# Decay and beta projection of a hybrid encoder: high and low weights in one weight of 64 columns, two passes in place of three

## The chip, the core and the metric

The kernel runs on one core of a Trainium2 chip. The metric is device time: microseconds of one execution, median over runs. TensorE (PE in the profile) has two clock levels, 1.2 and 2.4 GHz; the granted clock of a stretch is shown as a share of the higher one. The other engines are VectorE (DVE), ScalarE (ACT), GpSimd (POOL) and SyncE (SP), which here issues most of the transfers.

## The reference

One trunk layer on 1024 tokens of width 1024, with 16 learned tokens put in front (1040 positions). What the change touches is `ab`, the 32 columns of the input projection that give decay and beta (two directions, 8 heads each):

```python
hn = rms_norm(h, norm_g)
proj = hn @ w_in
f_in, qkv, z, ab, gate_f, gate_d = jnp.split(proj, points, axis=-1)
...
a_f, b_f, a_b, b_b = jnp.split(ab.astype(jnp.float32), 4, axis=-1)
g_f = -jnp.exp(a_log_f) * jax.nn.softplus(a_f + dt_bias_f)
beta_f = jax.nn.sigmoid(b_f)
...
o_fwd = gated_delta_chunked(qp, kp, vp, pad_to_chunks(g_f), pad_to_chunks(beta_f))
```

Everything else (the convolved q, k and v of 8 heads, the chunked delta scan in both directions, the Fourier branch, the two output gates, the router and the mixture of experts) is computed after it and is not edited.

## The kernel before

**Numbers in two parts.** Activations and weights are kept as a rounded high part and a low part, the remainder (`xh`, `xl`, `wh`, `wl`). A product is the sum of three passes: high weight by high input, high weight by low input, low weight by high input. The weight is the stationary operand, so the output stands with its columns on partitions and the tokens along the free axis. One pass over the 1024 inputs is 8 matmuls of 128 rows each, so an output tile takes 24 matmuls. `load_w` (L192) fetches a weight; `split` (L862) makes `wh` with ScalarE (L863) and `wl` with VectorE (L864). `product` (L211) runs the 24 matmuls (all on L220) into a PSUM tile `proj` and calls an evacuation.

**norm1** (L139) loads nine tiles of x (16 learned tokens, then 8 times 128), normalises each (`hn`, L170, VectorE), transposes it on TensorE into PSUM tiles `tp` (L176), and copies these out as `xh` (L178, ScalarE) and `xl` (L179, VectorE). Beside that it runs two projections over the token ranges of `EARLY` (272, 384 and 384 columns): `ab`, with 32 output columns, evacuated by one ScalarE copy into `abT` (L148), and the first tile of k, with 128, evacuated into `pad` (L360). `gates` (L230) turns `abT` into decays and betas for the delta scan, which are written to memory (`dF`) and read back from there.

**The heads** (about 60 to 500 us) project the other tiles of q, k, v with `product`. A projected tile goes from PSUM into `pad` (L360, ScalarE), through a convolution of five taps (first tap L373 on ScalarE, the four others L377 on VectorE, two instructions each, into `acc`), and through SiLU (L350, L351) into `kraw`, `qT` or `vraw`. For each k tile, `k_front` squares and sums transposed blocks (L442), makes the root by a few tiny VectorE and GpSimd instructions (L98 to L109, `rk_y`), and scales them into `ktok` (L450, ScalarE); TensorE transposes these back (L460) and ScalarE copies them into `kT` (L461). `vtok` (L473) is the same for v and is stored by a transfer `dv` (L477), after which its buffer is used again. For each q tile ScalarE squares (`sqq`, L482) and TensorE sums over partitions (L485). `decay` (L489) loads `F` from `dF` (L493), subtracts (L497) and limits it (L498) on VectorE, and takes its exponential on ScalarE (L499); `chunks` (L504) multiplies k by k or q by k (L511). Parts of the triangular inverses (`tmp`, `M`: L691, L693 on VectorE, `M<-dL` transfers L532) run among them.

**What sets the order.** A scheduler places instructions on each engine by its own model of time, outside the delta scan whose TensorE order is written by hand. Each engine then runs its list strictly in order. So fewer or other instructions in norm1 also change the order of instructions that nobody edited. The later parts are the scan (about 500 to 1040 us), projections of the output with router (to about 1250 us, L870 on TensorE) and the experts (weights fetched at L1233 on the SP queue).

Of the kernel before, what the change touches and what calls it, by code (L numbers as in the profile page):

```python
# [8 lines left out]
F32 = mybir.dt.float32  # L9
F32R = mybir.dt.float32r  # L10
BF16 = mybir.dt.bfloat16
I32 = mybir.dt.int32
AF = mybir.ActivationFunctionType
OP = mybir.AluOpType
# [81 lines left out]
def rsqrt(nc, pool, src, shape, scale, eps, tag):  # L96
    x = pool.tile(shape, F32, name=tag + "_x")
    nc.vector.tensor_scalar(x, src, scale, eps, op0=OP.mult, op1=OP.add)  # L98
    return rsqrt_of(nc, pool, x, shape, tag)
# [13 lines left out]
class Kern:  # L113
# [25 lines left out]
    def norm1(self, hp):  # L139

        tc, nc, io = self.tc, self.nc, self.io
        self.xh = hp.tile([128, 8, NT], F32R, name="xh")
        self.xl = hp.tile([128, 8, NT], F32R, name="xl")
        abT = self.tp.tile([32, NT], F32, name="abT", tag="pad")
        pad, ev_k = self.pad_tile()

        def ev_ab(a, b, o):
            nc.scalar.activation(abT[:, a:b], o, AF.Copy)  # L148
        with tc.tile_pool(name="n1", bufs=2) as wp, tc.tile_pool(name="n1p", bufs=self.TB, space=PSUM) as pp:
            xs = []  # L150
            for i in range(9):
                x = wp.tile([128, D], F32, name="x", bufs=9)
                src = io["meta_tokens"] if i == 0 else io["x"][128 * (i - 1):128 * i]
                nc.sync.dma_start(x[:src.shape[0]], src)
                xs.append(x)
                if i == 1:
                    g = wp.tile([128, D], F32, name="g1", bufs=1)
                    nc.scalar.dma_start(g, io["norm1_g"].partition_broadcast(128))
                    nc.gpsimd.dma_start(self.cst[:, :128], io["cst"][:, :128])
                if i == self.JB:  # L160
                    jobs = [(self.load_w(io["w_ab"], 8, 32), 32, ev_ab), (self.load_w(io["w_t"][12], 8, 128), 128, ev_k)]
            for i in range(9):
                n = 16 if i == 0 else 128
                x = xs[i]
                sq = wp.tile([128, D], F32, name="sq", bufs=1)
                ss = wp.tile([128, 1], F32, name="ss")
                nc.scalar.activation(sq[:n], x[:n], AF.Square, accum_out=ss[:n])
                r = rsqrt(nc, wp, ss[:n], [n, 1], 1.0 / D, EPS, "r")
                hn = wp.tile([128, D], F32, name="hn", bufs=self.HB)
                nc.vector.scalar_tensor_tensor(hn[:n], x[:n], r, g[:n], op0=OP.mult, op1=OP.mult)  # L170
                c0 = 0 if i == 0 else 16 + 128 * (i - 1)
                for b in range(2):
                    ps = pp.tile([128, 4, 128], F32, name="tp")
                    for j in range(4):
                        k = 4 * b + j
                        nc.tensor.transpose(ps[:, j, :n], hn[:n, 128 * k:128 * k + 128], self.ident[:n, :n])  # L176
                    oh = self.xh[:, 4 * b:4 * b + 4, c0:c0 + n]
                    nc.scalar.activation(oh, ps[:, :, :n], AF.Copy)  # L178
                    nc.vector.tensor_tensor(self.xl[:, 4 * b:4 * b + 4, c0:c0 + n], ps[:, :, :n],  # L179
                                            oh.bitcast(F32), op=OP.subtract)  # L180
            nc.sync.dma_start(self.cst[:, 128:], io["cst"][:, 128:])
            for r in range(3):
                for w, m, ev in jobs:
                    for _ in self.product(w, m, self.EARLY[r:r + 1], ev):
                        pass
        return abT, pad
# [7 lines left out]
    def load_w(self, src, kt, n):  # L194
# [5 lines left out]
        self.split(wh[:, :kt, :n], wl[:, :kt, :n], wr[:, :kt, :n])  # L200
        return wh, wl

    def project(self, *a):
        for _ in self.project_g(*a):
            pass
# [4 lines left out]

    def product(self, w, n, tiles, evac):  # L211
        nc = self.nc
        wh, wl = w
        for a, b in tiles:
            ps = self.pproj.tile([128, 512], F32, name="proj")
            o = ps[:n, :b - a]
            m = 0
            for k in range(8):
                for w, x in ((wh, self.xh), (wh, self.xl), (wl, self.xh)):
                    nc.tensor.matmul(o, w[:, k, :n], x[:, k, a:b], start=(m == 0), stop=(m == 23))  # L220
                    m += 1
                    if m == 24:
                        evac(a, b, o)
                    yield (b - a) / 2.4

# [1558 lines left out]
```

## Time and profile before

| | |
|---|---|
| time, median of 3 runs | 1783.92 us (1782.64 to 1784.94) |
| profiled execution: its time | 1784.23 us |
| profiled execution: its span | 1782.4 us |
| mean granted TensorE clock | 0.98 |
| busy: PE | 1709.2 us, 96% of the span, 10018 matmuls |
| busy: DVE | 1043.3 us, 59% |
| busy: ACT | 693.9 us, 39% |
| busy: POOL | 195.0 us, 11% |

The span runs from the first to the last instruction; 1.83 us of the profiled execution lie around it. PE counts matmuls, PEld the loads of their stationary operand, which run beside the matmuls. Busy shares are means over stages of very different character: a gain in one stage is read from that stage.

### The profile page before, as it was taken

How to read it: one execution, taken by the hardware profiler on the slowest of the kernel's cores; microseconds unless marked ns; L12 is line 12 of the kernel's file. 1: busy time of each engine (PE TensorE's matmuls, PEld its weight loads, DVE VectorE, ACT ScalarE, POOL GpSimd, SP SyncE). 2: the span in 40 equal slices, each digit the busy share in tenths (PEclk: the TensorE clock that was granted, in tenths of full speed). 3: DMA queues.
4: the chain of work that ended last, by engine and by line, in shares of the span. 5: the costliest groups of instructions: out<-in, count | busy, mean ns of one | idle time of the engine just before them, and what ended most of it. 6: DMA issues, size and time to landing. Idle time of an engine off the chain costs nothing. (4 is left out here: it accounts for less than half of the span.)

```text
span 1782.4 us, 26489 instructions
## 1 busy us (share of the span) xinstructions
PE 1709.2 (96%) x10018; PEld 1222.1 (69%) x10018; DVE 1043.3 (59%) x2198; ACT 693.9 (39%) x1537; POOL 195.0 (11%) x300
## 2 busy tenths in 40 slices
PE   7999999999999997999999999999699999999996
PEld 6999999999788885667666678888443444344342
DVE  6666699999458974565656546623624344424434
ACT  5666575553322113444444433322323333223232
POOL 2000000100100011132332000010201011101100
PEclk9999999999999998999999999999799999999998
DMA  4144643544653458343444067525699999999994
GB/s 162 48 136 158 184 130 131 154 134 135 226 154 130 159 195 219 113 143 101 142 142 123 23 220 249 176 89 202 248 397 420 414 420 418 419 419 415 420 419 192
DMA packets 118670, 391.16 MB, mean 219 GB/s; under 512 B 36439, under 2 KB 38399, under 8 KB 93567
## 3 DMA queue, kind: packets, MB, share of 16 engines
q1 hardware_dynamic: 102312, 337.65, 51.8%
q0 software_dynamic: 14736, 51.02, 9.0%
q8 instruction: 81, 1.33, 0.3%
q10 hardware_dynamic: 1488, 0.73, 0.2%
q14 instruction: 53, 0.43, 0.1%
HBM read 328.28 MB, written 65.26 MB: 221 GB/s over the span
## 5 line engine op out<-in xcount | busy, mean ns | idle before, releaser
L220 PE MATMUL proj<-xh,wh 128*128 128x346 f32 (+5 forms) x1080 | 389.9, 361 | 8.3 <-ACT zt L1699 6.0
L220 PE MATMUL proj<-xl,wh 128*128 128x346 f32 (+4 forms) x1080 | 390.4, 362 | 0.0
L220 PE MATMUL proj<-xh,wl 128*128 128x346 f32 (+4 forms) x1080 | 389.2, 361 | 0.0
L220 PEld LDWEIGHTS proj<-xh,wh 128*128 128x128 f32 (+1 forms) x1080 | 203.7, 189 | 28.2 <-ACT zt L1699 6.4
L220 PEld LDWEIGHTS proj<-xl,wh 128*128 128x128 f32 (+1 forms) x1080 | 203.7, 189 | 18.7 <-issue 5.8
L220 PEld LDWEIGHTS proj<-xh,wl 128*128 128x128 f32 (+1 forms) x1080 | 203.2, 188 | 19.1 <-issue 6.6
L377 DVE SCALAR_TENSOR_TENSOR acc<-pad,convw,acc 128x520 f32<-128x520 f32 x192 | 135.5, 753 | 17.0 <-ACT acc L373 16.9
L863 ACT ACTIVATE wh<-wr 128x1024 fp32r<-128x1024 f32 (+2 forms) x77 | 77.5, 1008 | 144.9 <-PE proj L220 84.0
L864 DVE TENSOR_TENSOR wl<-wr,wh 128x1024 fp32r<-128x1024 f32 (+2 forms) x77 | 88.9, 1156 | 50.5 <-ACT wh L863 42.5
L1346 DVE SCALAR_TENSOR_TENSOR ea<-ea,gw,gu 128x256 f32<-128x256 f32 x32 | 15.4, 481 | 172.4 <-ACT ea L1345 172.4
L691 DVE TENSOR_TENSOR tmp<-M 128x62 f32<-128x62 f32 (+30 forms) x124 | 106.0, 855 | 4.2 <-DMA M<-dL 2.6
L693 DVE TENSOR_TENSOR M<-M,tmp 128x62 f32<-128x62 f32 (+30 forms) x124 | 106.0, 855 | 1.9
L744 DVE SCALAR_TENSOR_TENSOR R<-main,egn,svtok 128x128 f32<-128x128 f32 x128 | 44.9, 351 | 101.5 <-PE main L742 101.5
L753 ACT ACTIVATE vd<-main,vdec 128x128 f32<-128x128 f32 x128 | 46.9, 366 | 137.8 <-PE main L751 137.6
L761 DVE SCALAR_TENSOR_TENSOR S<-S,egl,dS 128x128 f32<-128x128 f32 x240 | 72.6, 344 | 40.2 <-PE dS L760 39.6
L742 PE MATMUL main<-S,skq 128*64 128x128 f32 x1024 | 86.2, 288 | 0.1
L1345 ACT ACTIVATE ea<-gu 128x256 f32<-128x256 f32 x32 | 12.3, 384 | 183.7 <-PE gu L1341 183.7
L1371 DVE TENSOR_TENSOR yl<-dn,yh 128x512 fp32r<-128x512 f32 x64 | 44.2, 691 | 60.4 <-ACT yh L1370 60.3
L1370 ACT ACTIVATE yh<-dn 128x512 fp32r<-128x512 f32 x64 | 38.1, 595 | 97.8 <-PE dn L1368 97.1
L742 PEld LDWEIGHTS main<-S,skq 128*64 128x64 f32 x1024 | 54.7, 137 | 31.0 <-DVE so L764 16.9
L1341 PE MATMUL gu<-ml,gx 128*64 128x512 f32 x288 | 70.7, 607 | 3.6 <-DMA ml<-in_w_gu_dram 3.6
L1341 PE MATMUL gu<-mh,gx 128*64 128x512 f32 x288 | 67.0, 593 | 1.9 <-DMA mh<-in_w_gu_dram 1.9
(432 smaller groups left out, 3147.2 us busy)
## 6 DMA issues: line engine op xcount, KB each, us to landing
mh<-in_w_gu_dram SPq DMA_DIRECT2D x36, 1024.0 KB, 19.7
ml<-in_w_gu_dram SPq DMA_DIRECT2D x36, 1024.0 KB, 21.0
wr<-in_w_t_dram SPq DMA_DIRECT2D x52, 512.0 KB, 3.9
wx<-in_w_gu_dram SPq DMA_DIRECT2D x20, 1024.0 KB, 19.5
mh<-in_w_dn_dram SPq DMA_DIRECT2D x20, 1024.0 KB, 21.1
ml<-in_w_dn_dram SPq DMA_DIRECT2D x18, 1024.0 KB, 19.9
yh<-in_w_gu_dram SPq DMA_DIRECT2D x16, 1024.0 KB, 19.8
yl<-in_w_gu_dram SPq DMA_DIRECT2D x16, 1024.0 KB, 19.9
```

The lines of the kernel that those rows point to most:

```text
L220: nc.tensor.matmul(o, w[:, k, :n], x[:, k, a:b], start=(m == 0), stop=(m == 23))
L377: nc.vector.scalar_tensor_tensor(o, pad[:, a + j:a + j + NT // 2], w[:, j:j + 1], o, op0=OP.mult, op1=OP.add)
L691: nc.vector.tensor_tensor(tv, M[:, j + 1:, j:j + 1].to_broadcast([np_, m, j]), M[:, j:j + 1, :j].to_broadcast([np_, m, j]), op=OP.mult)
L693: nc.vector.tensor_tensor(M[:, j + 1:, :j], M[:, j + 1:, :j], tv, op=OP.add)
L742: nc.tensor.matmul(ps[hs[half], i], kv[:, i, 2 * (p % 4) + half], st[half], start=True, stop=True)
L744: nc.vector.scalar_tensor_tensor(R, ps[:, 0], self.egn[:, col:col + 1], d["vtok"][p // 4][:, p % 4], op0=OP.mult, op1=OP.add)
L753: nc.scalar.activation(vd, ps[:, 2], AF.Copy, scale=self.vdec[:, col:col + 1])
L761: nc.vector.scalar_tensor_tensor(st[half], st[half], self.egl[:, half, col:col + 1], dS, op0=OP.mult, op1=OP.add)
L863: self.nc.scalar.activation(hi, src, AF.Copy)
L864: self.nc.vector.tensor_tensor(lo, src, hi.bitcast(F32), op=OP.subtract)
L1341: nc.tensor.matmul(pg[self.HS[i]], d["x"][:, 4 * kk + k, c:c + 64], w[:, 4 * i + k], start=(kk == 0 and k == 0), stop=(kk == 1 and k == 3))
L1371: nc.vector.tensor_tensor(yl[:, cs], pd, yh[:, cs].bitcast(F32), op=OP.subtract)
```

## The change

`ab` gets one weight of 64 columns, the 32 high parts on the left and the 32 low parts on the right. Two passes over it (high input, low input) leave high weight by input on PSUM partitions 0 to 31 and low weight by input on 32 to 63. ScalarE copies the first half as before, and VectorE adds the second half. The sum has one small term more than before, low by low. Per token range 16 matmuls with 64 output columns take the place of 24 with 32.

```diff
         def ev_ab(a, b, o):
-            nc.scalar.activation(abT[:, a:b], o, AF.Copy)
+            nc.scalar.activation(abT[:, a:b], o[:32], AF.Copy)
+            nc.vector.tensor_tensor(abT[:, a:b], abT[:, a:b], o[32:], op=OP.add)
...
-                    jobs = [(self.load_w(io["w_ab"], 8, 32), 32, ev_ab), (self.load_w(io["w_t"][12], 8, 128), 128, ev_k)]
+                    jobs = [(self.load_ab(), 64, ev_ab), (self.load_w(io["w_t"][12], 8, 128), 128, ev_k)]
...
+    def load_ab(self):
+        w = self.wp.tile([128, 8, 128], F32R, name="wh")
+        self.wp.tile([128, 8, 128], F32R, name="wl")
+        wr = self.wp.tile([128, 8, 128], F32, name="wr")
+        self.nc.sync.dma_start(wr[:, :, :32], self.io["w_ab"])
+        self.split(w[:, :, :32], w[:, :, 32:64], wr[:, :, :32])
+        return w,
...
     def product(self, w, n, tiles, evac):
-        wh, wl = w
+        parts = ((w[0], self.xh), (w[0], self.xl), (w[-1], self.xh))[:1 + len(w)]
...
-                for w, x in ((wh, self.xh), (wh, self.xl), (wl, self.xh)):
-                    nc.tensor.matmul(o, w[:, k, :n], x[:, k, a:b], start=(m == 0), stop=(m == 23))
+                for wk, x in parts:
+                    nc.tensor.matmul(o, wk[:, k, :n], x[:, k, a:b], start=(m == 0), stop=(m == 8 * len(parts) - 1))
```

Line numbers of the changed kernel are one higher from L149 on and ten higher from about L204 on: L220 becomes L230, L377 L387, L450 L460, L482 L492, L497 L507 and so on. Its lists have 24 TensorE instructions fewer and 3 VectorE instructions more, and the scheduler's order differs on all engines up to about 500 us; from there on the lists are practically the same.

**TensorE, the first instructions of norm1.** `tp` are transposes of x, `proj` the projections. Before:

```order
L176 MATMUL tp<-cst,hn 128x16 x8
L176 MATMUL tp<-cst,hn 128x128 x24
L220 MATMUL proj<-xh,wh 32x272
L220 MATMUL proj<-xl,wh 32x272
L220 MATMUL proj<-xh,wh 128x272
L220 MATMUL proj<-xl,wh 128x272
L176 MATMUL tp<-cst,hn 128x128 x8
L220 MATMUL proj<-xh,wl 32x272
```

Now:

```order
L177 MATMUL tp<-cst,hn 128x16 x8
L177 MATMUL tp<-cst,hn 128x128 x32
L230 MATMUL proj<-xh,wh 64x272
L230 MATMUL proj<-xl,wh 64x272
...
L230 MATMUL proj<-xh,wh 128x272
L230 MATMUL proj<-xl,wh 128x272
L230 MATMUL proj<-xh,wl 128x272
```

The transposes of the fifth tile of x moved ahead of all projections, and the projection of `ab` has 64 output columns and no third pass.

**VectorE, ahead of the third k tile of the heads** (about 160 to 167 us before). The rows end with `km` (L451, now L461), which is beside `ktok` the first use of `rk_y`. Before:

```order
L498 TENSOR_TENSOR F<-F,cst 128x1024
L106 TENSOR_TENSOR rk_t<-rk_y 128x9
L497 TENSOR_TENSOR F<-PL,F 128x1024
L864 TENSOR_TENSOR wl<-wr,wh 128x1024
L107 TENSOR_TENSOR rk_t<-rk_t,rk_x 128x9
L498 TENSOR_TENSOR F<-F,cst 128x1024
L108 TENSOR_SCALAR rk_t<-rk_t 128x9
L109 TENSOR_TENSOR rk_y<-rk_y,rk_t 128x9
L451 TENSOR_SCALAR km<-prep,rk_y 16x128
L377 SCALAR_TENSOR_TENSOR acc<-pad,convw,acc 128x520 x8
```

Now:

```order
L508 TENSOR_TENSOR F<-F,cst 128x1024
L106 TENSOR_TENSOR rk_t<-rk_y 128x9
L507 TENSOR_TENSOR F<-PL,F 128x1024
L107 TENSOR_TENSOR rk_t<-rk_t,rk_x 128x9
L508 TENSOR_TENSOR F<-F,cst 128x1024
L108 TENSOR_SCALAR rk_t<-rk_t 128x9
L109 TENSOR_TENSOR rk_y<-rk_y,rk_t 128x9
L461 TENSOR_SCALAR km<-prep,rk_y 16x128
L874 TENSOR_TENSOR wl<-wr,wh 128x1024
L387 SCALAR_TENSOR_TENSOR acc<-pad,convw,acc 128x520 x8
```

The low part of a weight (L864, now L874) moved from ahead of the root to behind it. On TensorE, 23 matmuls of 346 columns stand between the last blocks before this place and the first L460, where 42 stood.

**ScalarE and SP around a sum of squares of q** (about 205 to 229 us before). On the SP queue, before:

```order
L520 DMA dQK<-F 128x1024
L532 DMA M<-dL 32x64x64 x3
L493 DMA F<-dF 64x1024 x2
L477 DMA dv<-vtok 128x1024
L521 DMA dkq<-qT 128x1024
```

Now:

```order
L530 DMA dQK<-F 128x1024
L542 DMA M<-dL 32x64x64 x2
L487 DMA dv<-vtok 128x1024
L503 DMA F<-dF 64x1024 x2
L531 DMA dkq<-qT 128x1024
```

The store of `vtok` moved ahead of the two loads of `F`. On ScalarE, before:

```order
L473 ACTIVATE vtok<-prep 128x512 x2
L350 ACTIVATE qT<-acc 128x8x64
L351 ACTIVATE qT<-acc 128x8x64
L499 ACT_TABLE_LOAD
L499 ACTIVATE F<-F 128x1024
L360 ACTIVATE pad<-proj 128x348
L482 ACTIVATE sqq<-qT 128x1024
```

Now:

```order
L483 ACTIVATE vtok<-prep 128x512 x2
L486 ACTIVATE vm<-prep 16x128
L360 ACTIVATE qT<-acc 128x8x64
L361 ACTIVATE qT<-acc 128x8x64
L370 ACTIVATE pad<-proj 128x348
L492 ACTIVATE sqq<-qT 128x1024
```

The square `sqq` moved ahead of the table load and the exponential of `F`. At a third place, about 345 to 360 us before, VectorE had the fourth pair of L377 of a v tile behind the subtraction L497; now all four pairs stand ahead of it. And on TensorE the back transposes of the last k tile (L460, now L470) and its products k by k (L511, now L521; at 373 us before) stood next to each other; now 19 matmuls of L230 stand between them.

## Rows read from the trace of the kernel before

**Rows 1.** Windows: us, busy us PE PEld DVE ACT POOL, clock, DMA share, GB/s

```profile
20.00:60.00 40.00, 40.00 (x264) 36.11 (x263) 27.39 (x58) 18.64 (x34) 3.24 (x7) 1.00 0.17 53
60.00:500.00 440.00, 432.92 (x3078) 412.81 (x3077) 338.69 (x533) 247.39 (x525) 27.41 (x60) 0.98 0.48 149
1500.00:1700.00 200.00, 194.40 (x873) 82.31 (x869) 79.37 (x149) 64.35 (x121) 18.79 (x16) 0.99 1.01 418
```

**Rows 2.** Timeline of the SP queue: start, us, what it issued

```profile
1228.85 28.85 SPq L981 DMA_DIRECT2D dh<-h  x3
1257.80 1.22 SPq L1233 DMA_DIRECT2D mh<-in_w_gu_dram  x2
```

**Rows 3.** Timeline of PE in norm1: start, us, one matmul each

```profile
30.24 0.34 PE L220 MATMUL proj<-xh,wh 128*32 128x384 f32 x1
...
31.80 0.33 PE L220 MATMUL proj<-xh,wh 128*32 128x384 f32 x1
...
44.62 0.34 PE L220 MATMUL proj<-xl,wh 128*128 128x384 f32 x1
...
47.24 0.34 PE L220 MATMUL proj<-xl,wh 128*128 128x384 f32 x1
```

**Rows 4.** Groups by line and shape, 18 to 48 us: busy us, mean ns

```profile
L170 DVE SCALAR_TENSOR_TENSOR hn<-x,r_y,g 128x1024 f32<-128x1024 f32 x5 | 6.4, 1278 | 0.0
...
L220 PEld LDWEIGHTS proj<-xl,wh 128*128 128x128 f32 x26 | 5.0, 194 | 0.1
...
L220 PEld LDWEIGHTS proj<-xh,wh 128*32 128x32 f32 x24 | 2.7, 111 | 1.0
```

**Rows 5.** Groups by line and shape, whole span

```profile
L1371 DVE TENSOR_TENSOR yl<-dn,yh 128x512 fp32r<-128x512 f32 x64 | 44.2, 691 | 60.4 <-ACT yh L1370 60.3
...
L764 DVE TENSOR_TENSOR so<-so,main 128x128 f32<-128x128 f32 x128 | 35.9, 280 | 1.9 <-PE main L763 1.6
```

**Rows 6.** Waits of PE, 60 to 500 us: us in total, times, longest

```profile
PE proj L220 <- ACT pad L360: 2.2, 1, 2.2
PE prep L460 <- ACT ktok L450: 2.2, 3, 1.4
PE prep L485 <- ACT sqq L482: 2.1, 1, 2.1
PE prep L511 <- ACT kT L461: 0.6, 1, 0.6
```

**Rows 7.** Windows of 10 us behind three of these waits

```profile
230.00:240.00 10.00, 10.00 (x72) 9.87 (x73) 10.00 (x17) 4.12 (x6) 0.13 (x2) 0.66 0.48 171
...
360.00:370.00 10.00, 10.00 (x56) 10.00 (x55) 10.00 (x15) 5.27 (x12) 0.00 (x0) 0.85 0.27 86
370.00:380.00 10.00, 9.40 (x109) 8.72 (x107) 8.91 (x11) 6.82 (x11) 0.14 (x2) 0.84 0.49 159
```

**Rows 8.** Timeline at the third k tile, all engines

```profile
162.76 1.23 DVE L497 TENSOR_TENSOR F<-PL,F 128x1024 f32<-128x1024 f32 x1 [2.24 <-DMA F<-dF]
...
163.91 1.22 DVE L864 TENSOR_TENSOR wl<-wr,wh 128x1024 fp32r<-128x1024 f32 x1
...
167.74 0.33 PE L460 MATMUL prep<-cst,ktok 128*128 128x128 f32 x1 [1.37 <-ACT ktok L450]
```

**Rows 9.** Timelines of SP and ACT ahead of the sum of squares

```profile
213.44 3.03 SPq L493 DMA_DIRECT2D F<-dF  x2
216.52 0.58 SPq L477 DMA_DIRECT2D dv<-vtok  x1
...
223.43 1.09 ACT L473 ACTIVATE vtok<-prep 128x512 f32<-128x512 f32 x2 [4.50 <-DMA dv<-vtok]
...
228.17 1.05 ACT L482 ACTIVATE sqq<-qT 128x1024 f32<-128x1024 f32 x1
```

**Rows 10.** Timeline at the v tile, DVE and ACT

```profile
353.95 1.23 DVE L497 TENSOR_TENSOR F<-F,G 128x1024 f32<-128x1024 f32 x1 [2.13 <-DMA F<-dF]
...
355.88 0.22 ACT L381 ACTIVATE vraw<-acc 128x16 f32<-128x16 f32 x1 [8.47 <-DVE acc L377]
```

More of the change, by code (lines that the diff above doesn't have):

```diff
@@ L218, in product @@
             for k in range(8):
-                for w, x in ((wh, self.xh), (wh, self.xl), (wl, self.xh)):
-                    nc.tensor.matmul(o, w[:, k, :n], x[:, k, a:b], start=(m == 0), stop=(m == 23))
+                for wk, x in parts:
+                    nc.tensor.matmul(o, wk[:, k, :n], x[:, k, a:b], start=(m == 0), stop=(m == 8 * len(parts) - 1))
                     m += 1
-                    if m == 24:
+                    if m == 8 * len(parts):
                         evac(a, b, o)
```

## Prediction

> **What bounds the kernel now.** I read the windows first. From 20 to 60 us, where the two projections of norm1 run, PE is busy 40.00 of 40 us; over the heads, 60 to 500 us, it is busy 432.92 of 440 us at a granted clock of 0.98 [rows 1]. So in the first 500 us a TensorE instruction taken out is time taken out, as long as PE finds its next operand ready. VectorE, the next engine, has 40 − 27.39 = 12.6 us of idle time in the first of these windows and 440 − 338.69 = 101 us in the second.
>
> The second question is whether an earlier end of the TensorE part reaches the end of the program. The experts run on the weight stream: from 1500 to 1700 us the DMA engines are full (1.01, 418 GB/s) [rows 1]. That stream doesn't start at a time of its own. On the SP queue the fetches of L1233 are issued at 1257.80 us, right behind the stores of h, on which the queue stood from 1228.85 us for 28.85 us [rows 2]; these stores come from the projections before the router. If everything ahead of them ends 3 us sooner, the stream starts 3 us sooner. I carry a saving of the heads to the end unchanged.
>
> The third view is the waits of PE in the heads: 7.1 us in six waits, four of which matter, 2.2 on `pad`, 2.1 on `sqq`, 1.4 on `ktok` and 0.6 on `kT` [rows 6]. Three of them are followed by a stretch at the lower clock. In a window of 10 us with mean clock c, half speed costs 10 × (1 − c) us of work: 3.4 us behind `sqq` (0.66), 1.5 behind `pad` (0.85), 1.6 behind `kT` (0.84) [rows 7], 6.5 in all. The 1.4 us wait on `ktok` lies in a stretch that the windows show without a loss of this size. Waits and clock together cost 7.1 + 6.5 = 13.6 us, over three times what the change removes. That is why the order matters as much as the removed work.
>
> **Removed matmuls.** A pass fewer is 8 matmuls per token range: 8 of 272 columns and 16 of 384. On PE the start of one 32x384 matmul follows the start of the one before by (31.80 − 30.24) / 9 = 0.173 us [rows 3] (the durations of 0.33 overlap and are no price). By the share of columns a 272 one is 0.173 × 272/384 = 0.123 us. Removed: 16 × 0.173 + 8 × 0.123 = **3.75 us**.
>
> **64 columns instead of 32.** The 48 remaining matmuls get wider. With 128 output columns the step is (47.24 − 44.62) / 15 = 0.175 us [rows 3], 1.4 ns above that of 32 columns, though a load of 128 columns is recorded at 194 ns and one of 32 at 111 [rows 4]. So the width costs between 0 and 48 × 1.4 ns = 0.07 us; I take nothing. What hides the load is the matmul in front of it.
>
> By the Trainium skill (TensorE: Matmul & The Clock Gate, section LDWEIGHTS) a load takes about its columns divided by 1.2 ns, so 64 columns take 27 ns more than 32; if loads set the pace, 48 of them would give back 1.3 us, and the removed work would be worth 2.45 us in place of 3.75. The rows of PE agree that wider loads last longer, but not that they set the step here.
>
> **Three adds on VectorE.** The trace has no add of this shape. The nearest are 0.280 us (128x128 with PSUM) and 0.691 us (128x512) [rows 5]; three cost 0.8 to 2.1 us. They lie in VectorE's 12.6 idle us and cost PE nothing by themselves. Without that cover they would cost at most the 2.1. What stands behind them on VectorE is `hn` and `xl` of the later tiles of x, which PE waits for.
>
> **norm1 in its new order.** The transposes of the fifth tile of x now stand ahead of all projections, so PE can't fill the time until `hn` with four early matmuls. One `hn` takes 1.278 us [rows 4]. Now PE loses nothing between 20 and 60 us [rows 1]; then it waits between 0 and one `hn`. I take the middle, **+0.7**.
>
> **Third k tile.** Now PE waits 1.37 us for `ktok` at 167.74 [rows 8]. Two moves act here. The low part of a weight (163.91, 1.22 us, on VectorE [rows 8]) goes behind the root, so `ktok` comes 165.04 − 163.91 = 1.1 us sooner. And 23 matmuls stand in front of L460 on PE where 42 stood: 19 × 0.175 × 346/384 = 3.0 us. The wait becomes 1.4 + 3.0 − 1.1 = 3.3 us, **+1.9**. Longer than any of the waits behind which the clock fell, it should cost clock as well: between 0 (as behind the 1.4 now) and 3.4; I take that of the two smaller cases, **+1.6**.
>
> **Sum of squares.** At 229.27 us PE waits 2.1 us for `sqq` [rows 6]. Back along the chain: `sqq` begins at 228.17, late because `vtok` began at 223.43 after 4.50 us of waiting for the store `dv` of the tile before; that store was issued on SP at 216.52, behind two loads of `F` that held the queue from 213.44 for 3.03 us [rows 9]. In the new order `dv` is issued ahead of these loads, and `sqq` stands ahead of the table load and the exponential. Each alone is worth more than the wait. What is late next are the loads of `F` and its exponential, which have some microseconds until the products that use them. I take wait and clock as gone: −2.1 − 3.4 = **−5.5**.
>
> **Late v tile.** At 358 us PE waits 2.2 us for `pad`. ScalarE was held for 8.47 us by the convolution, whose last pair stood behind a subtraction that waited 2.13 us for its transfer [rows 10]. With the four pairs ahead of the subtraction this goes: −2.2 − 1.5 = **−3.7**. For the last k tile, 19 matmuls (about 3.0 us) now cover the copy of `kT` into its place, on which PE waited 0.6: −0.6 − 1.6 = **−2.2**.
>
> **New stalls.** The order differs everywhere up to 500 us, and I could follow only the places that stall now. The same kinds of wait (a transfer of `F`, the root, `sqq`) will arise elsewhere. Their cost is between 0 and what it is today, 13.6 us; I take half, **+6.8**.
>
> **Sum.** −3.75 + 0.7 + 1.9 + 1.6 − 5.5 − 3.7 − 2.2 + 6.8 = −4.15. The profiled execution took 1784.23 us (a span of 1782.4 and 1.83 around it) and becomes 1780.1; it lies 0.31 above the median, so the median becomes **1779.8 us**. No new stalls would give 1773.0, as many as now 1786.6.
>
> **Rivals.** *Shift:* stalls come out as large as they were and only the work counts: −3.75 + 0.7 = −3.05, 1780.9. For it: the same scheduler with the same model; against it: two of the three costly causes are visibly taken apart. *Eaten:* the third k tile stalls longer as above, and the waits at 229 and 358 us stay, since other work holds the same buffers: −3.05 + 3.5 = +0.45, 1784.4. For it: the wait on `dv` is one on a queue, and the queue's other transfers remain. *Slower:* at the third k tile the first link is a transfer: L497 waited 2.24 us for `F<-dF` [rows 8]. With PE and VectorE earlier but the transfer not, or 2.2 us later, PE waits 3.3 + 2.1 = 5.4 us (+4.0) and loses 3.4 of clock, while the other two waits stay: −3.05 + 4.0 + 3.4 = +4.35, 1788.3. It decides once the wait passes 4.6 us: 4.6 − 1.4 + 3.4 − 3.05 = 3.55. *Loads set the pace:* were every step as much longer as the recorded load, 194 − 111 = 83 ns for 96 more columns or 28 ns for 32, 48 × 28 ns = 1.3 us of the shift would go, 1782.2; the equal steps of rows 3 speak against it.
>
> **Chances and range.** About 0.2% (3.6 us) is what a measurement of this kernel can tell from no change, so faster means below 1780.35 and slower above 1787.5. Forecast 0.55: by the half that I gave to new stalls 0.41 of it faster, 0.12 same, 0.02 slower. Shift 0.17 (0.08 faster, since its 1780.9 lies on the bound). Eaten 0.17, same. Loads 0.03, same. Slower 0.08. Faster 0.49, same 0.41, slower 0.10. The range leaves out the slower rival and the ends of the forecast where nearly no or nearly all stalls return: 1773.5 to 1785.5.
>
> **What would show it.** In the profile after: 24 matmuls fewer in norm1, with steps of 0.173 and 0.123 us as before; three adds of 0.3 to 0.7 us; PE busy nearly all of 20 to 60 us; a wait on `ktok` of about 3.3 us near 162 us; no wait on `sqq` near 226 us and none on `pad` near 355 us, with a clock of 1.00 behind both. I am wrong if the steps of the 64-column matmuls are longer, if the waits in the heads sum to much more or less than some 8 us, or if the heads end sooner and the stream of expert weights doesn't start sooner by the same.

## The result, and the profile after

The changed kernel takes 1793.30 us (median of 21 runs, 1783.18 to 1803.01) where the kernel before takes 1783.22 (21 runs, 1779.25 to 1789.27): ratio 1.0056, 95% interval 1.0043 to 1.0068. It is slower by about 10 us, where 1779.8 and a range up to 1785.5 had been predicted. The profiled execution took 1790.39 us with a span of 1788.6, so it is 2.9 us faster than the median; its rows show 6.2 us more than before, some six tenths of the difference of the medians.

What the prediction said of the matmuls and adds of norm1 is there, but not the whole gain. The timeline of TensorE in norm1:

```profile
34.44 0.34 PE L230 MATMUL proj<-xh,wh 128*64 128x384 f32 x1
...
35.31 0.34 PE L230 MATMUL proj<-xl,wh 128*64 128x384 f32 x1
```

That is five steps of 0.174 us, the step of 32 and of 128 columns in [rows 3]. The groups by line and shape, 18 to 60 us (busy us, mean ns):

```profile
L230 PEld LDWEIGHTS proj<-xh,wh 128*64 128x64 f32 x24 | 3.9, 162 | 0.8 <-ACT xh L179 0.3
...
L149 DVE TENSOR_TENSOR abT<-abT,proj 32x384 f32<-32x384 f32 x2 | 1.1, 547 | 5.4 <-ACT abT L148 5.4
...
L149 DVE TENSOR_TENSOR abT<-abT,proj 32x272 f32<-32x272 f32 x1 | 0.4, 429 | 0.1
```

The load of 64 columns lasts longer than that of 32 (162 against 111 ns in [rows 4]) and sets no step; the adds cost 0.43 to 0.55 us each.

The gain can be read at the transposes of `abT`, which have the same work in front of them in both kernels, but for the change. Before:

```profile
21.90 0.29 PE L220 MATMUL proj<-xh,wh 128*32 128x272 f32 x1
22.03 0.29 PE L220 MATMUL proj<-xl,wh 128*32 128x272 f32 x1
...
48.84 0.19 PE L243 MATMUL prep<-cst,abT 32*16 32x32 f32 x1
```

After:

```profile
23.28 0.43 PE L230 MATMUL proj<-xl,wh 128*64 128x272 f32 x1
23.51 0.43 PE L230 MATMUL proj<-xh,wh 128*64 128x272 f32 x1
...
47.40 0.19 PE L253 MATMUL prep<-cst,abT 32*16 32x32 f32 x1
```

They come 1.44 us sooner, where 3.05 had been forecast. A step of 272 columns takes 0.227 us in the changed kernel up to 24.4 us and 0.125 us behind it: up to there TensorE runs at the lower of its two levels. In the kernel before, the step is down to 0.13 us from 21.90 us on, some 2.5 us earlier. Before that rise TensorE had worked without a pause since 17.4 us; in the changed kernel it stood 0.71 us up to 19.96 us, for the root. But in e12 below, with the old instructions and no such pause, the step falls only at 23.25 us, so how much of the later rise is the change's own isn't shown. (The windows give the clock of 20 to 60 us as 1.00 in both kernels; the steps don't agree with that.)

The waits of TensorE from 60 to 500 us, and from 470 us to the scan:

```profile
PE prep L470 <- ACT ktok L460: 6.7, 3, 3.9
PE proj L230 <- ACT zt L1709: 2.4, 1, 2.4
```

```profile
PE proj L230 <- ACT zt L1709: 10.5, 3, 6.2
PE four L880 <- ACT yh L873: 2.3, 1, 2.3
PE proj L230 <- DVE wl L874: 2.0, 1, 2.0
```

In [rows 6] the heads had waits on `pad`, `sqq` and `kT`; these three are gone. In their place stand 6.7 us on `ktok`, 3.95 of them at the last k tile. The second list is news: in the kernel before, the same view of 470 to 690 us has one row, 6.0 us for `zt` right before the scan, and from 470 to 670 us none at all. Now there are four more waits there, 2.4 and 1.9 us for `zt`, 2.3 for `yh`, 2.0 for `wl`. The windows (columns as in [rows 1]) show it as busy time, before:

```profile
500.00:690.00 190.00, 183.99 (x900) 148.20 (x898) 150.03 (x205) 36.95 (x61) 9.88 (x15) 0.98 0.55 167
```

and after, with four windows of the heads above it:

```profile
140.00:150.00 10.00, 10.00 (x111) 9.50 (x110) 9.61 (x15) 4.84 (x23) 0.13 (x2) 0.83 0.53 159
160.00:170.00 10.00, 7.55 (x42) 7.03 (x41) 6.48 (x11) 8.38 (x18) 0.00 (x0) 0.83 0.39 134
305.00:315.00 10.00, 10.00 (x85) 9.85 (x86) 9.36 (x14) 3.45 (x21) 1.56 (x3) 0.83 0.43 112
365.00:375.00 10.00, 6.21 (x29) 5.20 (x31) 9.86 (x14) 6.25 (x15) 0.13 (x2) 0.83 0.43 158
500.00:690.00 190.00, 177.57 (x853) 143.81 (x853) 148.13 (x202) 36.69 (x59) 8.77 (x15) 0.98 0.52 163
```

TensorE is busy 177.57 of the 190 us from 500 us on where it was busy 183.99: 6.4 us lost in a stretch to which the prediction had given nothing. The delay reaches the end: on the SP queue the first expert weights are now fetched at 1264.32 us,

```profile
1264.32 1.21 SPq L1243 DMA_DIRECT2D mh<-in_w_gu_dram  x2
```

6.5 us later than in [rows 2], and the span is 6.2 us longer.

For the experiments two landmarks are useful, the state products of the learned tokens (`prep<-mvd,km`) at the end of the heads and the first product of the scan (`main<-S,skq`). Before they begin at 470.6 and 684.1 us, after at 469.7 and 691.8. So the heads end 0.9 us sooner, and the stretch behind them takes 222.1 us where it took 213.5; the four new waits there, 8.6 us together, make up the difference. These are single executions: e1 and e3 below hold one and the same order up to the first landmark and reach it at 465.6 and 469.7 us, so a difference of 4 us at that point says little. The time between the landmarks repeats better, within 2.5 us among the runs of the old order and within 1 among those of the new.

### The profile page after: what moved, and what is told of

Its sections match the earlier page's. It is cut to its first block, busy times and chain, and to the rows that moved or that the text cites. A ratio compares the mean times of both kernels' runs of the same rounds, so it can differ in the third digit from the quotient of the medians.

```text
span 1788.6 us, 26448 instructions
## 1 busy us (share of the span) xinstructions
PE 1707.8 (95%) x9994; PEld 1223.2 (68%) x9994; DVE 1044.1 (58%) x2201; ACT 691.6 (39%) x1536; POOL 191.8 (11%) x300
## 5 line engine op out<-in xcount | busy, mean ns | idle before, releaser
L230 PE MATMUL proj<-xh,wh 128*128 128x346 f32 (+5 forms) x1080 | 390.7, 362 | 10.6 <-ACT zt L1709 10.5
L230 PE MATMUL proj<-xl,wh 128*128 128x346 f32 (+4 forms) x1080 | 390.5, 362 | 0.2 <-DVE xl L180 0.2
L230 PE MATMUL proj<-xh,wl 128*128 128x346 f32 (+4 forms) x1056 | 383.1, 363 | 2.0 <-DVE wl L874 2.0
L230 PEld LDWEIGHTS proj<-xh,wh 128*128 128x128 f32 (+1 forms) x1080 | 204.8, 190 | 30.2 <-ACT zt L1709 11.6
L230 PEld LDWEIGHTS proj<-xl,wh 128*128 128x128 f32 (+1 forms) x1080 | 204.5, 189 | 18.3 <-issue 5.6
L230 PEld LDWEIGHTS proj<-xh,wl 128*128 128x128 f32 x1056 | 200.8, 190 | 21.2 <-issue 7.3
L387 DVE SCALAR_TENSOR_TENSOR acc<-pad,convw,acc 128x520 f32<-128x520 f32 x192 | 135.9, 751 | 16.1 <-ACT acc L383 16.1
L874 DVE TENSOR_TENSOR wl<-wr,wh 128x1024 fp32r<-128x1024 f32 (+1 forms) x76 | 88.4, 1163 | 46.1 <-ACT wh L873 46.1
```

The source lines that it names most:

```text
L230: nc.tensor.matmul(o, wk[:, k, :n], x[:, k, a:b], start=(m == 0), stop=(m == 8 * len(parts) - 1))
L387: nc.vector.scalar_tensor_tensor(o, pad[:, a + j:a + j + NT // 2], w[:, j:j + 1], o, op0=OP.mult, op1=OP.add)
L874: self.nc.vector.tensor_tensor(lo, src, hi.bitcast(F32), op=OP.subtract)
```

## The experiments

All runs but the two kernels of the study hold an order: a list of ranks gives, for each engine, the place of every instruction ahead of the scan, and an edge that fixes issue order (no waiting for completion) goes from each instruction to the next; the three adds alone are left free. The kernel's work is untouched by it. No run holds a kernel in its very own order, so what the edges cost by themselves isn't shown; e5, e6 and e9, which hold the new order but for one move, lie within 3 us of the changed kernel. The core of it:

```python
for i in nc.cur_bb.bb.instructions:          # traced ahead of the scan
    ...
    per.setdefault(str(i.engine).split(".")[-1], []).append(i)
for e, (t, lo, hi) in tables.items():
    ...
    flat = [i for r in order[lo:hi] for i in rows[r]]
    for a, b in zip(flat, flat[1:]):
        tc.add_manual_dep(b, a.name, mybir.DependencyInfo(mybir.DependencyClass.NoSync, mybir.DependencyReason.DATA), reason="held order")
```

"Old order" is that of the kernel before, "new order" that of the changed kernel. The results (ratios to the kernel before, run on the same chip; its medians lay between 1782.1 and 1783.1 us; the last column is the time between the two landmarks in the profile):

| run | kernel, order | median us | ratio, 95% interval | between landmarks |
|---|---|---|---|---|
| the change | new | 1793.30 | 1.0056 (1.0043 to 1.0068) | 222.1 |
| e1 | the change, old order | 1779.97 | 0.9984 (0.9972 to 0.9995) | 215.9 |
| e2 | before, new order | 1791.54 | 1.0049 (1.0031 to 1.0066) | 221.3 |
| e3 | the change, old to 470 us, then new | 1790.18 | 1.0041 (1.0027 to 1.0055) | 221.2 |
| e4 | the change, new to 470 us, then old | 1785.43 | 1.0020 (1.0005 to 1.0035) | 215.2 |
| e5 | new, root together | 1790.71 | 1.0043 (1.0030 to 1.0056) | 223.0 |
| e6 | new, evacuation before `mt` | 1791.80 | 1.0058 (1.0034 to 1.0082) | 226.1 |
| e7 | e5 and e6 | 1795.10 | 1.0061 (1.0038 to 1.0084) | 223.4 |
| e8 | the change, old order mended | 1775.39 | 0.9959 (0.9947 to 0.9972) | 215.7 |
| e9 | new, loads `M` later | 1790.75 | 1.0056 (1.0042 to 1.0070) | 222.5 |
| e10 | e6 and e9 | 1791.55 | 1.0055 (1.0041 to 1.0068) | 223.7 |
| e11 | e5, `ktok` before `pad` | 1791.01 | 1.0055 (1.0042 to 1.0068) | 221.9 |
| e12 | before, old order mended | 1779.47 | 0.9985 (0.9974 to 0.9995) | 214.2 |
| e13 | new to 470 us, then TensorE old, others free | 1796.19 | 1.0079 (1.0061 to 1.0097) | 228.7 |
| e14 | new to 470 us, then TensorE new, others free | 1787.40 | 1.0034 (1.0017 to 1.0052) | 220.8 |
| e15 | new, SP old behind 470 us | 1804.04 | 1.0116 (1.0097 to 1.0135) | 236.2 |

**Order or instructions?** The theory (A) was that the new instructions save what was predicted and the new order costs more; the rival (B), that the wider loads, the adds or the first matmul's wait for the weight's low part cost the time.

```diff
 # e1: the changed kernel                # e2: the kernel before
+ORDER = old ranks, all five engines     +ORDER = new ranks, all five engines
```

e1: 

> The change, with every instruction ahead of the delta scan kept in the order that the kernel before has on its engine (issue-order edges alone; the three new adds are left free). Theory A, the new order costs the time and the new instructions save theirs: 3.75 us of matmuls less and the old waits, so 1777 to 1782 us, faster than before by about 0.2%. Theory B, the new instructions themselves cost it (wider weight loads, the adds, the low parts of the weight that the first matmul now waits for): still about 1790 us or more, since they are all there.

e2: 

> The instructions of the kernel before (three passes, 32 columns, no add), in the order that the changed kernel has on every engine ahead of the scan; the 24 removed matmuls stand right behind the ones of the second pass. Theory A: the time of the changed kernel plus 3.75 us of matmuls, 1793 to 1799 us. Theory B: about 1783 us, the time of before.

Measured: 1779.97 us with the change in the old order, 1791.54 us with the old instructions in the new order. e1 lies where theory A put it. e2 is slow, as A said and against B, but 1.5 us under A's range and no slower than the changed kernel: the 24 matmuls more don't show in its time. B falls: all new instructions are in e1, and it is faster than before, while e2 has none of them and is slow. The one new wait that B had named is there and small. TensorE in e1, timeline:

```profile
20.32 0.49 PE L231 MATMUL proj<-xh,wh 128*64 128x272 f32 x1 [1.02 <-DVE wh L877]
```

The first matmul of `ab` waits 1.0 us for the low part, which now lies in the same tile as the high part. In the changed kernel's own order the transposes of the fifth tile come first and that wait isn't seen.

**Which stretch?** The split is at the first landmark.

```diff
 # e3                                    # e4
+ORDER = old ranks to 470 us, then new   +ORDER = new ranks to 470 us, then old
```

e3: 

> The change; up to the state products at 470 us (L671) all engines keep the order of the kernel before, behind it, up to the scan, the order of the changed kernel. In the profile after, waits and clock between 500 us and the scan cost 7.3 us more than before, and those ahead of it 2.6 us more. If theory A holds and that split is right: 1780 + 7 = 1785 to 1790 us. If the loss lies in the heads instead: about 1780 us.

e4: 

> The mirror: up to 470 us the order of the changed kernel, behind it the order of the kernel before, with the change. Theory A with the split of the profile: 1780 + 2.6 = 1780 to 1785 us. If the loss lies in the heads: 1787 us or more. If the loss needs both parts together (late data from the heads, and an order that doesn't forgive it), both this and its mirror stay near 1780.

Both come out as theory A said, some tenths of a microsecond above the upper ends of its ranges. Against e1 the new order costs 10.2 us behind 470 us (e3) and 5.5 us ahead of it (e4). The sum, 15.7, is a little above the 13.3 us between e1 and the changed kernel, within what the intervals allow. So the split of the profile was right in its sense, and both parts were larger than one execution had shown. The waits of TensorE from 470 us to the scan in e3 are those of the changed kernel:

```profile
PE proj L231 <- ACT zt L1712: 8.3, 3, 5.3
PE proj L231 <- DVE wl L877: 2.0, 1, 2.0
PE four L883 <- ACT yh L876: 1.6, 1, 1.6
PE four L883 <- DVE gt L1704: 0.3, 1, 0.3
```

In e4, in the same view from 300 us on, the wait of the last k tile stays, and of the late ones only `gt` is left, beside the one on `zt` right before the scan, which was 6.0 us in the kernel before:

```profile
PE proj L231 <- ACT zt L1712: 6.5, 1, 6.5
PE prep L473 <- ACT ktok L463: 5.0, 1, 5.0
PE four L883 <- DVE gt L1704: 0.9, 2, 0.5
```

**The wait on `ktok` at the last k tile.** In the changed kernel the rows of ScalarE and VectorE at this place are

```profile
367.48 0.16 DVE L109 TENSOR_TENSOR rk_y<-rk_y,rk_t 128x9 f32<-128x9 f32 x1
```

```profile
367.67 0.81 ACT L370 ACTIVATE pad<-proj 128x348 f32<-128x348 f32 x2 [1.89 <-DVE rk_y L109]
```

and `ktok` follows at 368.37. Read so, the tiny root instructions, each behind a full-size one on VectorE, are what is late. e5 moves them:

```diff
 # VectorE, new order
 L106 TENSOR_TENSOR rk_t<-rk_y 128x9
+L107, L108, L109
 L507 TENSOR_TENSOR F<-F,G 128x1024
 ...
-L107 ... L108 ... L109, each four or five rows further down
```

> The changed kernel in its own order with one move: for the last k tile, three tiny instructions of the root (L107, L108, L109) stand right behind L106 on VectorE; in the changed kernel each stands behind a full-size subtraction, elimination or convolution. In the profile after, PE waits 3.95 us there for ktok and then 1.7 us are lost at the lower clock. If the scattered root is what is late: that wait falls under 1 us and the kernel comes out 3 to 6 us under the changed one, 1787 to 1790 us. If ktok is held by something else (ScalarE, the sums of squares): the wait stays near 4 us and the time near 1793 us.

The wait did not go (4.9 us), and the time is 1790.71. The root now ends at 355 us, and the same row of ScalarE reads

```profile
366.55 0.81 ACT L373 ACTIVATE pad<-proj 128x348 f32<-128x348 f32 x2 [2.82 <-DVE acc L390]
```

So it was the convolution: the evacuation writes a `pad` that VectorE's last taps (L390) still read. In the changed kernel L109 followed these taps on VectorE, and the profile put the wait down to the one that came last. e11 then takes `ktok` out from behind the evacuations:

```diff
 # ScalarE, on top of e5
+L460 ACTIVATE ktok<-prep,rk_y 128x128 x8
 L370 ACTIVATE pad<-proj 128x348
 L370 ACTIVATE pad<-proj 128x346
-L460 ACTIVATE ktok<-prep,rk_y 128x128 x8
```

> The changed kernel in its own order; for the last k tile the root stands together as before, and on ScalarE the eight ktok stand ahead of the two evacuations into pad, which wait for VectorE's convolution. If only the order on ScalarE holds ktok: the wait of 3.9 to 4.9 us on ktok falls under 1.5 us and nothing takes its place, 1788 to 1790 us. If VectorE's convolution is what is late: PE waits for pad a microsecond later instead, with 3 us or more, and the time stays at 1791 us or more.

TensorE's waits from 300 to 470 us in e11:

```profile
PE prep L473 <- ACT ktok L463: 1.2, 1, 1.2
PE proj L231 <- ACT pad L373: 1.0, 1, 1.0
PE prep L485 <- ACT vraw L364: 0.7, 1, 0.7
```

The wait on `ktok` fell to 1.2 us as its first theory said, two others of 1.0 and 0.7 appeared, and the median, 1791.01, with its ratio of 1.0055, is not to be told from the changed kernel's. Of the two expectations neither is met in full: less took its place than the second said, and yet the stretch behind began at 469.6 us as in the changed kernel (469.7).

**The waits behind 470 us.** The rows of the changed kernel's ScalarE and SP there:

```profile
481.80 0.57 ACT L1709 ACTIVATE zt<-proj 128x512 f32<-128x512 f32 x1
481.92 16.21 SPq L542 DMA_DIRECT2D M<-dL  x4
...
483.23 0.58 ACT L1709 ACTIVATE zt<-proj 128x512 f32<-128x512 f32 x1
...
500.83 0.85 SPq L1710 DMA_DIRECT2D dz<-zt  x2
...
505.69 0.60 ACT L1709 ACTIVATE zt<-proj 128x512 f32<-128x512 f32 x1 [3.77 <-DMA dz<-zt]
```

Four loads of the second inverse hold the SP queue for 16.2 us; the stores of two `zt`, ready at 482 and 484 us, go out at 500.8; a later `zt` waits for its buffer, and TensorE for it. In the kernel before, the same loads are issued at 495.9, behind most stores. Three runs move single things:

```diff
 # e6: ScalarE                           # e9: SP queue
-L550 ACTIVATE mt<-M (fourth)            -L542 DMA M<-dL x4
 L1709 ACTIVATE zt<-proj                  L1710 DMA dz<-zt x2
 L873 ACTIVATE wh<-wr                     L200 DMA wr<-in_w_t_dram
 L1709 ACTIVATE zt<-proj                  L595 DMA fT<-dfr
+L550 ACTIVATE mt<-M (fourth)            +L542 DMA M<-dL x4
```

e6: 

> The changed kernel in its own order with one move on ScalarE: the fourth copy mt of the first inverse, which waits 2.9 us for a transfer, goes behind the two evacuations zt (L1709) and the weight's high part that follow it. In the profile after, PE waits 2.4 us at 480 us for zt. If the copy is what holds the evacuation: that wait goes and 2 to 4 us are saved, 1789 to 1791 us. If PE is then late for the next thing as well (the waits at 504 and 579 us grow): about 1793 us.

e7 (with the root of e5): 

> Both moves together. If the two stalls add up: 6 to 9 us under the changed kernel, 1784 to 1787 us, near the kernel before. If a saving ahead is eaten by a later wait: no better than the better one of the two.

e9: 

> The changed kernel in its own order with one move on the SP queue: the four loads M<-dL of the second inverse (L542, issued from 481.9 us for 16.2 us in the profile after) go behind the two stores dz, a weight load and a load of fT that stood behind them. If these loads hold the stores, and by them the buffers zt and PE: the wait on zt at 504 us (1.9 us) goes, the weight comes 14 us sooner, and 2 to 5 us are saved, 1788 to 1791 us. If the queue is not what holds PE: 1793 us.

e10 (e6 and e9): 

> The same move together with that of the copy mt on ScalarE, which by itself moved the wait from 480 us to 500 us, where it became 6.6 us. If the loads on SP are the cause behind both: no wait of over 1 us from 475 to 510 us, and 4 to 7 us saved, 1786 to 1789 us. If the waits move on to the next product (579 us, 657 us): 1790 us or more.

The moves of e6, e9 and e10 did to their own waits what they should. None moved the time by more than the intervals. In e6 the wait at 480 us went and the next one grew: TensorE stood 6.6 us at 500 us, in this row of its timeline,

```profile
506.95 0.79 PE L231 MATMUL proj<-xh,wh 128*128 128x512 f32 x1 [6.62 <-ACT zt L1712]
```

since the stores still stood behind the loads. In e9 the wait at 504 us went, those at 479, 577 and 656 us stayed, and the one on `zt` right before the scan was 6.9 us, 0.7 more than in the changed kernel. e7 kept 5.0 us on `ktok` and has 4.4 us on `zt` at 507 us; neither of its expectations' savings came. In e10, with e6 and e9 together, the waits of over a microsecond from 470 to 670 us are

```profile
PE chan L611 <- DVE AB L616: 3.1, 1, 3.1
PE four L883 <- ACT yh L876: 3.1, 1, 3.1
PE proj L231 <- DVE wl L877: 1.8, 1, 1.8
```

where the 3.1 on `chan` is new. The stretch between the landmarks stayed at 222 to 226 us in all of them. The expected savings were wrong: a wait removed in the new order came back at another place, whole (e6) or in part (e9, e10).

**Whose order?** With the cause behind 470 us open, three more runs split it by engine.

```diff
 # e13: new to 470 us, then TensorE in the old order, the other engines free
 # e14: new to 470 us, then TensorE in the new order, the other engines free
 # e15: all new, only SP in the old order behind 470 us
```

e13: 

> The change; up to 470 us the changed kernel's order on all engines; behind it, up to the scan, TensorE in the order of the kernel before, all other engines as the scheduler places them around that. If TensorE's order is what costs the time there: near the mirror run with the whole old order behind 470 us (1785.4 us), so 1784 to 1788 us. If another engine's order does: 1790 us or more.

e14: 

> The same with TensorE in its new order behind 470 us, all other engines as the scheduler places them. If TensorE's order costs the time: 1790 us or more, as the changed kernel. If SP's or ScalarE's order does, and comes out otherwise here: under 1788 us.

e15: 

> The changed kernel in its own order, with SP alone in the old order behind 470 us (the second inverse's loads then stand behind the stores dz and the weights). If the queue's order costs the time: 1784 to 1788 us. If TensorE's order does: 1790 us or more.

e13's median is above the changed kernel's and e14's below it (1787.4), against the theory that TensorE's own order costs the time. Neither is proof: the intervals of both overlap that of the changed kernel, and e14's stretch takes 220.8 us, as with the whole new order. e15, with SP alone in the old order, is clearly slower. And e13 is no clean case: around the old TensorE order the other engines came out with a wait of their own, the only one of over a microsecond from 470 to 670 us,

```profile
PE chan L611 <- DVE EO L602: 11.8, 1, 11.8
```

and e15 has one of 10.5 us at the same kind of product. What they show together is that neither TensorE's nor SP's old list by itself makes the stretch fast; those of ScalarE, VectorE and GpSimd were not tried alone. The whole old order takes 213.5 to 216 us between the landmarks (before, e1, e4, e8, e12), the whole new order 221 to 222 (the change, e2, e3), and lists from both, mixed by engine, up to 236.

**The causes that the prediction had read in the old order.** e8 is the change in the old order with the three moves that the prediction had credited to the new order; e12 is the kernel before with the same three.

```diff
 # VectorE, late v tile
-L497 TENSOR_TENSOR F<-F,G
 L377 SCALAR_TENSOR_TENSOR acc<-pad,convw,acc x2
+L497 TENSOR_TENSOR F<-F,G
 # ScalarE, ahead of the sum of squares
-L499 ACT_TABLE_LOAD
-L499 ACTIVATE F<-F
 L360 ACTIVATE pad<-proj 128x348
 L482 ACTIVATE sqq<-qT
+L499 ACT_TABLE_LOAD
+L499 ACTIVATE F<-F
 # SP
+L477 DMA dv<-vtok
 L493 DMA F<-dF x2
-L477 DMA dv<-vtok
```

e8: 

> The change in the order of the kernel before, with three moves that the new order had suggested and on which the prediction rested: the last pair of the convolution of the late v tile ahead of the subtraction L497 (VectorE), the square of q ahead of the table load and the exponential (ScalarE), and the store dv ahead of the two loads of F (SP). In the old-order run PE waited 2.9 us for pad at 350 us, followed by 1.7 us of clock, and 0.9 us for sqq. If these causes were read rightly: both waits go, 1773 to 1778 us, 0.3 to 0.5% under the kernel before. If other work takes their place: about 1780 us.

e12: 

> The kernel before (three passes, 32 columns), in the mended old order of the run before with the three moves. If the three moves are worth what the waits showed, 4 to 5 us: 1778 to 1780 us, and the change is worth 3 to 4 us on top (1775.4 with it). If the change is worth more or less where no stall stands behind it, the difference to 1775.4 says how much.

e8 takes 1775.39 us, ratio 0.9959 (0.9947 to 0.9972), the fastest of all runs and faster than both kernels. Its waits from 60 to 500 us are

```profile
PE prep L473 <- ACT ktok L463: 0.8, 1, 0.8
PE prep L524 <- ACT kT L474: 0.6, 1, 0.6
```

1.4 us where the kernel before had 7.1 in [rows 6]. The three moves are worth 1779.97 − 1775.39 = 4.6 us with the change (e1, e8) and, by the ratio 0.9985, some 2.6 us without it (e12), less than the 4 to 5 expected; the change is worth 1779.47 − 1775.39 = 4.1 us in the mended order (4.6 by the ratios, since the two ran on different chips) and 3.2 us in the old one. In the new order it is worth nothing that can be told: 1793.30 with it and 1791.54 without (e2), with intervals that overlap.

## Why the prediction was wrong

**The removed matmuls: the price of a step right.** −3.75 us and 0.7 for norm1, −3.05 together; in a held old order the change measures −3.2 (e1) and −4.1 us (e8 against e12). That these totals fit so well may in part be luck: in the profile of e1 the transposes of `abT` come only 1.1 us sooner than in the kernel before (47.72 against 48.84), so the rest was gained elsewhere. 64 columns cost nothing, by the steps of 0.174 us; the three adds cost 0.43 to 0.55 us each, inside the bounds of [rows 5], and no wait of TensorE for them shows. By the Trainium skill (TensorE: Matmul & The Clock Gate, section LDWEIGHTS) loads grow with their columns, by an estimate of 27 ns from 32 to 64 columns. The trace agrees that they grow, but by 51 ns there (111, 162 and 194 ns for 32, 64 and 128 columns), and the equal steps show that loads don't set the pace here. So nothing of the 1.3 us that they would have given back was lost.

**norm1: the wait right, a term missing.** The predicted 0.7 us showed as 0.7 of waiting for the root and 0.2 for `xl`. But the sum had no term for the clock at the start, since the windows showed 1.00 there. In its profiled execution the changed kernel works some 2 us longer at the lower level before the clock rises, which costs about 1 us (an estimate from the steps of 0.227 and 0.125 us). So 1.44 us came of the 3.05.

**Third k tile: right in kind.** Predicted were a wait of 3.3 us and 1.6 of clock; the profile has 2.45 and a window at 0.83, which is 1.7 by the same formula.

**Sum of squares and late v tile: the causes right, the gain not kept.** Both waits are gone as forecast, and e8, with the three moves together, has neither. But at the last k tile, where the prediction had put −2.2 since matmuls would cover `kT`, TensorE waits 3.95 us for `ktok`, one step earlier in the same chain, with a window at 0.83 behind it. VectorE is busy 9.86 of 10 us there. The heads end 0.9 us sooner, where −3.05, +3.5 and −11.4 had been on paper ahead of the term for new stalls.

**New stalls: the step that failed.** "The order differs everywhere up to 500 us ... Their cost is between 0 and what it is today, 13.6 us; I take half." In the heads its size was a little small. In the profile they hold 9.1 us of waits and four windows at 0.83, 6.8 us by the formula. Of these 15.9 us, 4.2 are the third k tile's, which had a term of its own, and 2.4 are the wait on `zt` at 480 us, behind the heads; the 9.3 left are inside the bounds of 0 and 13.6 and 2.5 above the half. What failed is that the term ended at 500 us. The sentence ahead of the prediction, that the lists are practically the same from there on, is mistaken: they differ up to the scan, at about 690 us, and the stretch from 470 us, in which the kernel before has no wait up to 670 us, costs 8.6 us more in the profile. By e3 against e1 that stretch alone is worth 10.2 us, more than twice the whole change of −4.15 that was forecast. It got no term since the lists were taken to be the same; and that the old order had no stall there says nothing of what another order can add. By e4 against e1 the new order costs 5.5 us ahead of 470 us as well, where all terms of the sum but the −3.75 come to −0.4.

**The rivals.** The one on the slower side stood at 1788.3 with a chance of 0.08 and put the loss in one wait at the third k tile. The right side, the wrong place: most of the loss lies behind 470 us, and single moves in the new order that took a wait out saved nothing.

**What stays open.** Which rows of the new order cost the 8 to 10 us behind 470 us. The runs exclude the instructions themselves, show that the whole old order is fast there and the whole new one slow, and that neither the late copy `mt`, nor the second inverse's loads, nor TensorE's or SP's list is by itself the cause. The changed kernel's runs spread over 20 us, those of before over 10. Its spread goes with the granted clock, 0.986 in the fastest run (1783.18 us) and 0.973 in the slowest (1803.01); what lowers the clock in some runs was not tried.

## What to carry to other kernels

Where a scheduler places the instructions, an edit of a few microseconds can be a new draw of the whole order; its price can't be read from the stalls that the old order has, least of all where it has none. Hold the old order, measure the edit in it, and only then mend the order, place by place: here that turned 10 us lost into 7.0 us gained (e8: 1775.39 beside 1782.42 for the kernel before on the same chip). And a stall that is taken out need not save time, since the wait can come back further on: of the moves in e5, e6, e9, e10 and e11, all but e5's took out or shortened the wait that they aimed at, and none moved the end.

## What the runs showed of the hardware

Four loads `M<-dL` held the SP queue for 16.2 us in the changed kernel, against 8.8 us when issued 14 us later in the kernel before; what stood behind them on the queue, two stores, a weight and a load of `fT`, was issued 16 to 20 us later than before. What made the same four loads hold it twice as long isn't shown.

The clock can fall to its lower level without a wait of TensorE: from 305 to 315 us it was busy 10.00 of 10 us at a mean of 0.83, where 300 to 310 us of the kernel before shows 1.00. Ahead of it TensorE had run a group of short matmuls, in the changed kernel

```profile
303.30 1.15 PE L521 MATMUL prep<-kT 128*64 128x64 f32 x32
304.38 1.95 PE L495 MATMUL prep<-ones,sqq 128*128 128x1 f32 x16
```

and the same group stands ahead of the other busy window at 0.83, 140 to 150 us. The group alone does not bring the fall: in the kernel before it runs at 308.15 us and the clock stays at 1.00. At the start of the kernel the clock rises at a time that differs between executions: the step of 272 columns fell from 0.227 to 0.125 us at about 21.8 us in the kernel before, 23.2 in e12 and 24.5 in the changed kernel.

And the name of a releaser can mislead: the one that the profile gave for `pad` at 367.67 us (L109) was only the last to come; with it moved away (e5), the convolution stood in the same row and the wait of TensorE behind it was still 4.9 us.
